# A two-layer decoder step: a 256-column matmul pair as one matmul of 512 columns

## The chip, the cores and the metric

The kernel runs on one core of one Trainium2 chip. The metric is the device time of one execution in microseconds: 1185.92 us for the kernel before (median of three runs, 1185.88 to 1188.42). All times below are from these runs and from one profiled execution.

## The reference

One inference step of a decoder with two layers: 512 prompt tokens and 8 sample tokens, 1024 channels. Layer 0 mixes tokens by attention in a window of 128, layer 1 by gated linear attention (GLA). Behind each mixer stand an output projection, a residual with layer norm, a gated feed-forward of 2816 channels with a causal convolution of width 3 on its gate half, and a second residual with layer norm. All in float32.

```python
def conv_ffn(x, buf, w_up, conv_w, conv_b, w_down):
    T = x.shape[1]
    h = x @ w_up
    a, u = h[..., :D_FF], h[..., D_FF:]
    ap = jnp.concatenate([buf.astype(a.dtype), a], axis=1)
    c = conv_b + sum(conv_w[j] * ap[:, j:j + T] for j in range(CONV_W))
    y = (jax.nn.gelu(c, approximate=False) * u) @ w_down
    return y, ap[:, T:]
...
x <- LayerNorm(ALPHA * x + mixer(x) @ w_o)
x <- LayerNorm(ALPHA * x + conv_ffn(x))
```

(The last two lines are the loop over the layers in short.) The feed-forward's weights, 1024x5632 and 2816x1024 a layer, are most of the arithmetic.

## The kernel before

Activations lie with channels on the 128 partitions and tokens along the row. The 520 tokens are two groups: a has the first 256 prompt tokens, b the other 256 and the 8 sample tokens (264). A float32 value is kept as a high and a low part in the matmul format (fp32r): xh and xl for the input of a projection, hh and hl for the hidden values or the mixer's output. Each such tile has, for each of 8 slices of 128 channels, two halves of a row of 128 (or 132) columns; `in_turn` hands the columns to the matmul one from each half in turn, and `parted` does the same split on the way in.

A weight is cut into units: 128 output channels by up to 1024 input channels. `load_unit` fetches a unit by DMA (512 KB) into raw, ACT makes its high part wh (L149), DVE its low part wl (L152). `product` (L155 to L167) is the core. For each slice k of a unit it issues three matmuls into one PSUM tile accp: wh with xh (L164), wh with xl (L165), wl with xh (L166), so a unit is 24 matmuls of 256 or 264 columns (18 in the first third of the down projection). There are four accp tiles (ACCS, L39), handed out in turn: a unit's matmuls wait until the unit four before it has been read out.

`order` (L870) sets the sequence of units: group a's and group b's units alternate, a ahead by four or five; at the start of a phase (a projection with its successors) a's first units therefore run alone. The tile framework places what each function emits on the engines in an order of its own, by a simulated timeline; on each engine that order is then fixed.

What reads the PSUM tiles:
- `out_proj` (L484) and the last third of `ffn_down` (L552) pass them to `ln_chunk` (L180): one DVE addition into the residual x (L189 or L191), a square on ACT and running sums for the layer norm. `ln_end` (L219) makes the mean and the reciprocal deviation r (L237), then for each slice u (DVE, L245), xh (ACT, L253), x (POOL, L254) and xl (DVE, L257).
- `ffn_gate` (L513): ACT copies the tile to aext (L523) and makes the first tap of the convolution from PSUM (L526); DVE adds the two other taps (L527, L528); ACT applies Gelu (L535).
- `ffn_value` (L539): DVE multiplies the gate with the PSUM tile into hprod (L543), and `split` (L169) makes hh (ACT, L170) and hl (DVE, L171).
- the other parts of `ffn_down`: one DVE addition into x (L556, L558).

The first units of a feed-forward are gate, value, gate, value and so on for group a, so the tile that the fifth unit needs is the first gate's.

Of the kernel before, what the change touches and what calls it, by code (L numbers as in the profile page):

```python
# [11 lines left out]
F32 = mybir.dt.float32  # L12
F32R = mybir.dt.float32r
I32 = mybir.dt.int32
AF = mybir.ActivationFunctionType
ALU = mybir.AluOpType
# [4 lines left out]
P = 128  # L21
D = 1024
KD = 8
# [48 lines left out]
def parted(rows):  # L72

    return rows.rearrange("p (j t) -> p t j", t=2)


def in_turn(rows):

    return rows.rearrange("p t j -> p j t")


class Group:
    def __init__(self, i):
        self.i = i
        self.n = 256 if i == 0 else 256 + NS
        self.c0 = 256 * i
        self.name = "ab"[i]


class Net:  # L90
    def __init__(self, tc, ctx, I, O):
        self.tc, self.nc, self.I, self.O = tc, tc.nc, I, O
        self.groups = [Group(0), Group(1)]
        self.stack = ctx
        pool = lambda name, bufs=1, **kw: ctx.enter_context(tc.tile_pool(name=name, bufs=bufs, **kw))
        self.const = pool("const")
        self.act = pool("act")
        self.raw = pool("raw", RAWS)
        self.wts = pool("wts", WSLOTS)
        self.ln = pool("ln")  # L100
        self.acc = pool("acc", ACCS, space=PSUM)
        self.mps = pool("mps", space=PSUM)
        self.dram = pool("dram", 2, space=DRAM)
        nc = self.nc
        c = self.const
        self.par = c.tile([P, NPAR], F32, name="par")
        self.ident = c.tile([P, P], F32, name="ident")
        self.ones_a = c.tile([P, P], F32, name="ones_a")
        nc.gpsimd.memset(self.ones_a, 1.0 / D)
        self.ones_c = c.tile([P, P], F32, name="ones_c")  # L110
        nc.gpsimd.memset(self.ones_c, 1.0 / P)
        self.eps = c.tile([P, 2], F32, name="eps")
        nc.gpsimd.memset(self.eps[:, 0:1], NORM_EPS)
        nc.gpsimd.memset(self.eps[:, 1:2], 1.0)
        for g in self.groups:
            s = [P, KD, g.n]
            g.x = self.act.tile(s, F32, name=f"x_{g.name}")

            s = [P, KD, 2, g.n // 2]
            g.xh = self.act.tile(s, F32R, name=f"xh_{g.name}")  # L120
            g.xl = self.act.tile(s, F32R, name=f"xl_{g.name}")
            g.hh = self.act.tile(s, F32R, name=f"hh_{g.name}")
            g.hl = self.act.tile(s, F32R, name=f"hl_{g.name}")
        self.units = []
        self.w = {}
# [29 lines left out]
    def product(self, g, u, rh, rl):  # L155
# [10 lines left out]
            nc.tensor.matmul(o, l[:, ks], xh, start=False, stop=k == nt - 1)  # L166
        return ps[:, :g.n]  # L167

    def split(self, hi, lo, src):  # L169
        self.nc.scalar.activation(hi, src, AF.Copy)  # L170
        self.nc.vector.tensor_tensor(lo, src, hi.bitcast(F32), op=ALU.subtract)  # L171
# [5 lines left out]
        return self.mps.tile([P, 512], F32, name=tag, bufs=2 if tag == "sc" else 1)  # L177


    def ln_chunk(self, g, m, ps, scaled):  # L180


        nc, n, x = self.nc, g.n, g.x
        t = lambda name: self.ln.tile([P, g.n], F32, name=f"{name}_{g.name}")
        c = lambda name, b=1: self.ln.tile([P, NT - 256], F32, name=name, bufs=b)[:, :n]
        if m:
            yield 0
        if scaled:
            nc.vector.tensor_tensor(x[:, m], x[:, m], ps, op=ALU.add)  # L189
        else:  # L190
            nc.vector.scalar_tensor_tensor(x[:, m], x[:, m], ALPHA, ps, op0=ALU.mult, op1=ALU.add)  # L191
        if m == 0:
            yield 1
            mp = self.mtile("sc")[:, :n]
            nc.tensor.matmul(mp, self.ones_c, x[:, 0], start=True, stop=True)
            sb = c("sb")
            nc.scalar.copy(sb, mp)
            sa = sb
            if not scaled:
                sa = c("sa")  # L200
                nc.scalar.activation(sa, mp, AF.Copy, scale=1.0 / ALPHA)
            for i in range(KD):
                eng = nc.gpsimd if i else nc.vector
                eng.tensor_tensor(x[:, i], x[:, i], sa if i else sb, op=ALU.subtract)
            g.s2 = t("s2")
            nc.scalar.activation(g.s2, x[:, 0], AF.Square)
            return
        q = c("sq", 2)
        sq = nc.scalar.activation(q, x[:, m], AF.Square)
        if m == 6 and g.i == 0:  # L210
            with self.tc.issue_after(sq.ins):
                nc.scalar.preload_act_table_set("natural_log_exp_and_others")
        if m == 1:
            g.s1 = t("s1")
        nc.vector.tensor_tensor(g.s1, x[:, 0] if m == 1 else g.s1, x[:, m], op=ALU.add)
        eng = nc.gpsimd if m < S2P else nc.vector
        eng.tensor_tensor(g.s2, g.s2, q, op=ALU.add)
# [264 lines left out]


    def out_proj(self, g, u, m, i):  # L484
        ps = self.product(g, u, g.hh, g.hl)
        yield from self.ln_chunk(g, m, ps, False)
        if m == KD - 1:
            yield from self.ln_end(g, i)

# [22 lines left out]

    def ffn_gate(self, g, u, layer, j, q):  # L513
        nc, n = self.nc, g.n
        ps = self.product(g, u, g.xh, g.xl)
        w = lambda i: self.par[:, C_CW + (layer * 3 + i) * NF + j:C_CW + (layer * 3 + i) * NF + j + 1]
        cb = self.par[:, C_CB + layer * NF + j:C_CB + layer * NF + j + 1]
        a = self.fp.tile([P, 2 + NT - 256], F32, name="aext", bufs=2)
        if g.i == 0:
            nc.gpsimd.memset(a[:, 0:2], 0.0)  # L520
        else:
            self.pcopy(a[:, 0:2], self.hist[:, j])
        nc.scalar.copy(a[:, 2:2 + n], ps)  # L523
        t = lambda name: self.fp.tile([P, NT - 256], F32, name=name, bufs=2)
        c = t("conv")
        nc.scalar.activation(c[:, :256], ps[:, :256], AF.Identity, scale=w(2), bias=cb)  # L526
        nc.vector.scalar_tensor_tensor(c[:, :256], a[:, 1:257], w(1), c[:, :256], op0=ALU.mult, op1=ALU.add)  # L527
        nc.vector.scalar_tensor_tensor(c[:, :256], a[:, 0:256], w(0), c[:, :256], op0=ALU.mult, op1=ALU.add)  # L528
        if g.i == 0:
            self.pcopy(self.hist[:, j], a[:, 256:258])  # L530
        else:
            nc.vector.scalar_tensor_tensor(c[:, 256:n], a[:, 258:2 + n], w(2), self.base[:, j], op0=ALU.mult, op1=ALU.add)
            self.pcopy(self.nconv_p[:, j], a[:, 256:258])
            self.pcopy(self.nconv_s[:, j, :, 1], a[:, 258:2 + n])
        nc.scalar.activation(c[:, :n], c[:, :n], AF.Gelu)  # L535
        g.gate = c
        yield 0

    def ffn_value(self, g, u, layer, j, q):  # L539
        nc, n = self.nc, g.n  # L540
        ps = self.product(g, u, g.xh, g.xl)
        h = self.fp.tile([P, NT - 256], F32, name="hprod", bufs=2)
        nc.vector.tensor_tensor(h[:, :n], g.gate[:, :n], ps, op=ALU.mult)  # L543
        self.split(g.hh[:, q], g.hl[:, q], parted(h[:, :n]))
        if g.i and j == NF - 1:
            nc.scalar.dma_start(out=self.O["conv_p"][layer], in_=self.nconv_p)
            nc.scalar.dma_start(out=self.O["conv_s"][layer], in_=self.nconv_s)
            self.close(self.fp_cm)
            self.fp = None
        yield 0  # L550

    def ffn_down(self, g, u, layer, part, m):  # L552
        nc = self.nc
        ps = self.product(g, u, g.hh, g.hl)
        if part == 0:
            nc.vector.scalar_tensor_tensor(g.x[:, m], g.x[:, m], ALPHA, ps, op0=ALU.mult, op1=ALU.add)  # L556
        elif part == 1:
            nc.vector.tensor_tensor(g.x[:, m], g.x[:, m], ps, op=ALU.add)  # L558
        else:
            yield from self.ln_chunk(g, m, ps, True)  # L560
            if m == KD - 1:
                yield from self.ln_end(g, 2 * layer + 1, last=layer == 1)


    def gla_open(self):
# [473 lines left out]
```

## Time and profile before

| | kernel before |
|---|---|
| runs | 1188.42, 1185.88, 1185.92 us |
| profiled execution | 1187.92 us, span 1185.1 us |
| PE busy | 1127.1 us (95%), 9598 matmuls |
| DVE busy | 777.6 us (66%) |
| ACT busy | 556.0 us (47%) |
| POOL busy | 362.0 us (31%) |
| mean granted clock of PE | 0.982 of full speed |

The span runs from the first to the last recorded instruction; the execution is longer by 2.8 us. A matmul's recorded duration overlaps the next one's, so the pace is read from start to start. PEclk is the granted clock: 1.00 is 2.4 GHz, 0.50 is 1.2 GHz. In a timeline the number in brackets is the time the engine stood idle before the instruction, and who released it.

### The profile page before, as it was taken

The numbers are of one execution on the slowest core, as the hardware profiler recorded it, in microseconds if no ns is written. First come the engines' busy times: TensorE is split into PE (matmuls) and PEld (weight loads), VectorE is DVE, ScalarE is ACT, GpSimd is POOL, SyncE is SP. The second block draws the span as 40 slices with busy tenths as digits, with TensorE's granted clock in tenths as the row PEclk, the third lists the DMA queues.
The fourth block names the chain that finished last, engine by engine and source line by source line (L and its number), as shares of the span: only waits on it lengthen the run. The fifth ranks groups of instructions, "written<-read, shape, count | busy, mean of one in ns | idle before, by whom it ended". The sixth has DMA issues, their size and how long they took to land.

```text
span 1185.1 us, 24433 instructions
## 1 busy us (share of the span) xinstructions
PE 1127.1 (95%) x9598; PEld 1088.0 (92%) x9598; DVE 777.6 (66%) x1649; ACT 556.0 (47%) x1222; POOL 362.0 (31%) x603
## 2 busy tenths in 40 slices
PE   8869989999999999999899999998999999999994
PEld 7768779899999999999799899898999999999994
DVE  7969878854555445558867678789645555355567
ACT  4447645643444234435555455456533443244433
POOL 5646676510011001147500000368210111011345
PEclk9989999999999999999899999999999999999997
DMA  7124013223323232332123553542323332323212
GB/s 224 58 82 138 2 27 123 72 81 116 108 90 108 90 107 90 107 118 95 54 72 95 160 174 121 169 127 90 94 85 119 95 107 90 107 90 107 73 61 72
DMA packets 49547, 118.57 MB, mean 100 GB/s; under 512 B 5753, under 2 KB 23321, under 8 KB 49433
## 3 DMA queue, kind: packets, MB, share of 16 engines
q1 hardware_dynamic: 47417, 115.41, 31.2%
q10 hardware_dynamic: 2016, 1.62, 0.4%
q8 instruction: 75, 1.23, 0.4%
q14 instruction: 39, 0.32, 0.1%
HBM read 108.54 MB, written 8.47 MB: 99 GB/s over the span
## 4 chain that ended last, share of the span: by engine, by line
PE 73%; DVE 12%; DMA 5%; POOL 4%; issue 3%; ACT 2%; SPq 0%; POOLq 0%; DVEq 0%; ACTq 0%
PE accp L165 22%; PE accp L164 22%; PE accp L166 22%; DMA raw<-in_w_qkv 2%; DMA vb<-dv 2%; DVE wl L152 2%; POOL x_b L254 1%; PE pv L445 1%; POOL x_a L254 1%; DVE u L245 1%; DVE qs L372 1%; DVE x_b L240 1%; DVE x_a L240 1%; PE sc L706 1%; PE pv L717 1%
## 5 line engine op out<-in xcount | busy, mean ns | idle before, releaser
L152 DVE TENSOR_TENSOR wl<-raw,wh 128x1024 fp32r<-128x1024 f32 (+2 forms) x189 | 229.1, 1213 | 142.1 <-ACT wh L149 131.6
L149 ACT ACTIVATE wh<-raw 128x1024 fp32r<-128x1024 f32 (+1 forms) x176 | 183.4, 1042 | 215.3 <-PE accp L165 191.8
L164 PE MATMUL accp<-xh_b,wh 128*128 128x264 f32 x976 | 273.5, 280 | 2.8 <-DVE hprod L543 2.8
L165 PE MATMUL accp<-xl_a,wh 128*128 128x256 f32 x976 | 271.4, 279 | 3.5 <-DVE xl_a L257 2.8
L166 PE MATMUL accp<-xh_a,wl 128*128 128x256 f32 x976 | 270.5, 278 | 3.0 <-DVE wl L152 3.0
L165 PE MATMUL accp<-xl_b,wh 128*128 128x264 f32 x976 | 272.8, 280 | 0.4 <-DVE xl_b L257 0.4
L164 PE MATMUL accp<-xh_a,wh 128*128 128x256 f32 x976 | 270.1, 279 | 3.2 <-ACT conv L526 1.4
L166 PE MATMUL accp<-xh_b,wl 128*128 128x264 f32 x976 | 272.1, 279 | 0.0
L165 PEld LDWEIGHTS accp<-xl_a,wh 128*128 128x128 f32 x976 | 187.7, 192 | 5.7 <-DVE xl_a L257 3.7
L164 PEld LDWEIGHTS accp<-xh_a,wh 128*128 128x128 f32 x976 | 187.1, 193 | 6.3 <-ACT conv L526 1.8
L166 PEld LDWEIGHTS accp<-xh_a,wl 128*128 128x128 f32 x976 | 188.1, 193 | 5.0 <-DVE wl L152 4.0
L164 PEld LDWEIGHTS accp<-xh_b,wh 128*128 128x128 f32 x976 | 186.7, 191 | 4.0 <-DVE hprod L543 3.2
L165 PEld LDWEIGHTS accp<-xl_b,wh 128*128 128x128 f32 x976 | 186.6, 191 | 1.9 <-issue 0.9
L166 PEld LDWEIGHTS accp<-xh_b,wl 128*128 128x128 f32 x976 | 186.1, 191 | 1.4 <-issue 1.3
L164 PE MATMUL accp<-hh_b,wh 128*128 128x264 f32 x480 | 133.4, 278 | 2.6 <-ACT hh_b L170 2.6
L165 PE MATMUL accp<-hl_b,wh 128*128 128x264 f32 x480 | 134.2, 280 | 0.0
L166 PE MATMUL accp<-hh_b,wl 128*128 128x264 f32 x480 | 133.3, 278 | 0.0
L165 PE MATMUL accp<-hl_a,wh 128*128 128x256 f32 x480 | 132.3, 276 | 0.3 <-DVE hl_a L171 0.3
L164 PE MATMUL accp<-hh_a,wh 128*128 128x256 f32 x480 | 132.2, 278 | 0.0
L166 PE MATMUL accp<-hh_a,wl 128*128 128x256 f32 x480 | 131.8, 275 | 0.0
L164 PEld LDWEIGHTS accp<-hh_b,wh 128*128 128x128 f32 x480 | 91.2, 190 | 3.1 <-ACT hh_b L170 2.9
L165 PEld LDWEIGHTS accp<-hl_a,wh 128*128 128x128 f32 x480 | 91.9, 192 | 1.3 <-issue 0.8
(304 smaller groups left out, 2095.6 us busy)
## 6 DMA issues: line engine op xcount, KB each, us to landing
raw<-in_w_up SPq DMA_DIRECT2D x88, 512.0 KB, 3.4
raw<-in_w_down SPq DMA_DIRECT2D x32, 512.0 KB, 3.5
raw<-in_w_gla SPq DMA_DIRECT2D x24, 512.0 KB, 3.5
raw<-in_w_mix_o SPq DMA_DIRECT2D x16, 512.0 KB, 3.9
raw<-in_w_down SPq DMA_DIRECT2D x16, 384.0 KB, 3.1
sgla<-in_state_gla SPq DMA_DIRECT2D x16, 256.0 KB, 2.8
vb<-dv SPq DMA_DIRECT2D x16, 256.0 KB, 3.9
out_gla_s<-sgla SPq DMA_DIRECT2D x16, 256.0 KB, 2.9
```

What stands on the lines that cost most here:

```text
L149: nc.scalar.activation(h[:, c], r[:, c], AF.Copy)
L152: nc.vector.tensor_tensor(l[:, c], r[:, c], h[:, c].bitcast(F32), op=ALU.subtract)
L164: nc.tensor.matmul(o, h[:, ks], xh, start=k == 0, stop=False)
L165: nc.tensor.matmul(o, h[:, ks], xl, start=False, stop=False)
L166: nc.tensor.matmul(o, l[:, ks], xh, start=False, stop=k == nt - 1)
L240: nc.vector.tensor_tensor(x[:, m], x[:, m], mu, op=ALU.subtract)
L245: nc.vector.tensor_tensor(u, x[:, m], r, op=ALU.mult)
L254: ts = nc.gpsimd.tensor_scalar(x[:, m], u, sc, bi, op0=ALU.mult, op1=ALU.add)
L372: nc.vector.tensor_tensor(qs[oth, v], r[own, :256], qs[own, v].bitcast(F32), op=ALU.subtract)
L445: nc.tensor.matmul(pv[64 * v:64 * v + 64, b * P:(b + 1) * P], self.vtok[:, kb, 64 * v:64 * v + 64], parts[v][w][:, b], start=i == 0, stop= ...
L706: nc.tensor.matmul(up, vks[b][:, 0:P], vks[b][:, P:], start=True, stop=True)
L717: nc.tensor.matmul(ob, att[:, b], vks[b][:, P:], start=first, stop=True)
```

## The change

For group a alone, in the output projections and the feed-forwards of both layers, the high and low parts lie side by side in one tile (xs_a, hs_a), and `product2` takes the place of `product`. For each slice it issues two matmuls: wh with both parts, 512 columns, into the whole PSUM tile, and wl with the high part, 256 columns, into the tile's first half. (The last slice has the two in the other order.) The second half of the tile then holds wh times the low part, and is added in a step of its own: in `ln_chunk` and `ffn_down` by another DVE addition into x; in `ffn_gate` by a DVE addition into aext, after which ACT reads aext in place of PSUM for the first tap; in `ffn_value` ACT copies it to hprod, DVE adds the other half, and the product with the gate follows. Group b, the attention's q, k and v and all GLA input projections keep `product`. The two halves that a matmul takes in turn now lie 1024 bytes apart in a row of xs_a or hs_a, where they were 512 bytes apart.

```diff
-        for g in self.groups:
+        for i, g in enumerate(self.groups):
...
+            if i == 0:
+                s = [P, KD, 2, 2, g.n // 2]
+                g.xs = self.act.tile(s, F32R, name=f"xs_{g.name}")
+                g.hs = self.act.tile(s, F32R, name=f"hs_{g.name}")
+                g.xh, g.xl = (g.xs[:, :, :, q] for q in range(2))
+                g.hh, g.hl = (g.hs[:, :, :, q] for q in range(2))
+                continue
...
+    def product2(self, g, u, rs, rh, rl):
+        if rs is None:
+            return self.product(g, u, rh, rl), None
+        nc = self.nc
+        h, l = self.w[u]
+        nt = self.units[u][1]
+        ps = self.acc.tile([P, 512], F32, name="accp")
+        o = ps.rearrange("p (j t) -> p j t", t=2)
+        for k in range(nt):
+            ks = slice(k * P, (k + 1) * P)
+            last = k == nt - 1
+            both = lambda: nc.tensor.matmul(o, h[:, ks], in_turn(rs[:, k].rearrange("p t q j -> p t (q j)")), start=k == 0, stop=last)
+            low = lambda: nc.tensor.matmul(o[:, :P], l[:, ks], in_turn(rh[:, k]), start=False, stop=False)
+            for f in (low, both) if last else (both, low):
+                f()
+        return ps[:, :256], ps[:, 256:]
...
@@ ln_chunk
+        if lo is not None:
+            nc.vector.tensor_tensor(x[:, m], x[:, m], lo, op=ALU.add)
@@ ffn_gate
-        ps = self.product(g, u, g.xh, g.xl)
+        ps, lo = self.product2(g, u, g.xs, g.xh, g.xl)
...
-        nc.scalar.activation(c[:, :256], ps[:, :256], AF.Identity, scale=w(2), bias=cb)
+        if lo is not None:
+            nc.vector.tensor_tensor(a[:, 2:2 + n], a[:, 2:2 + n], lo, op=ALU.add)
+        nc.scalar.activation(c[:, :256], ps[:, :256] if lo is None else a[:, 2:258], AF.Identity, scale=w(2), bias=cb)
@@ ffn_value
-        ps = self.product(g, u, g.xh, g.xl)
+        ps, lo = self.product2(g, u, g.xs, g.xh, g.xl)
         h = self.fp.tile([P, NT - 256], F32, name="hprod", bufs=2)
+        if lo is not None:
+            nc.scalar.copy(h[:, :n], lo)
+            nc.vector.tensor_tensor(h[:, :n], h[:, :n], ps, op=ALU.add)
+            ps = h[:, :n]
@@ ffn_down (parts 0 and 1)
+        if lo is not None:
+            nc.vector.tensor_tensor(g.x[:, m], g.x[:, m], lo, op=ALU.add)
```

In the changed kernel the lines stand lower: the addition of the gate is L557, of the value L577, the taps L559 and L560, and ln_end's r, u and xl are L267, L275 and L287.

The order on DVE at the start of layer 0's feed-forward, where group b's layer norm ends (r, u, xl_b) and the first gate (conv, aext) and value (hprod) units of group a come in; before:

```order
L237 SCALAR_TENSOR_TENSOR r<-msq,r 128x264
L245 TENSOR_TENSOR u<-x_b,r 128x264 x2
L527 SCALAR_TENSOR_TENSOR conv<-aext,par,conv 128x256 x2
L528 SCALAR_TENSOR_TENSOR conv<-aext,par,conv 128x256
L257 TENSOR_TENSOR xl_b<-x_b,xh_b 128x264
L245 TENSOR_TENSOR u<-x_b,r 128x264
```

And the same place on DVE in the changed kernel:

```order
L267 SCALAR_TENSOR_TENSOR r<-msq,r 128x264
L557 TENSOR_TENSOR aext<-aext,accp 128x256
L275 TENSOR_TENSOR u<-x_b,r 128x264 x2
L577 TENSOR_TENSOR hprod<-hprod,accp 128x256
L557 TENSOR_TENSOR aext<-aext,accp 128x256
L577 TENSOR_TENSOR hprod<-hprod,accp 128x256
L559 SCALAR_TENSOR_TENSOR conv<-aext,par,conv 128x256
```

The four additions that free PSUM tiles stand behind r now, and the taps behind them; before, DVE freed no tile here until hprod, further down, since ACT read the gates out.

The order on DVE at the start of layer 1's feed-forward, the same instructions of the same functions; before:

```order
L240 TENSOR_TENSOR x_b<-x_b,mu 128x264 x3
L235 TENSOR_TENSOR msq<-r 128x264
L236 SCALAR_TENSOR_TENSOR msq<-msq,nv 128x264
L237 SCALAR_TENSOR_TENSOR r<-msq,r 128x264
L245 TENSOR_TENSOR u<-x_b,r 128x264 x2
L527 SCALAR_TENSOR_TENSOR conv<-aext,par,conv 128x256 x2
L528 SCALAR_TENSOR_TENSOR conv<-aext,par,conv 128x256
```

And in the changed kernel:

```order
L270 TENSOR_TENSOR x_b<-x_b,mu 128x264 x3
L287 TENSOR_TENSOR xs_a<-x_a,xs_a 128x2x128 x2
L265 TENSOR_TENSOR msq<-r 128x264
L266 SCALAR_TENSOR_TENSOR msq<-msq,nv 128x264
L267 SCALAR_TENSOR_TENSOR r<-msq,r 128x264
L275 TENSOR_TENSOR u<-x_b,r 128x264 x2
L287 TENSOR_TENSOR xl_b<-x_b,xh_b 128x264
L275 TENSOR_TENSOR u<-x_b,r 128x264
L557 TENSOR_TENSOR aext<-aext,accp 128x256
```

The first gate's addition stands behind three u and an xl_b here, and the last two low parts of group a (xs_a) stand behind the x_b.

## Rows read from the trace of the kernel before

**Rows 1.** The page's table of busy time: engine, us, share, instructions.

```profile
PE 1127.1 (95%) x9598; PEld 1088.0 (92%) x9598; DVE 777.6 (66%) x1649; ACT 556.0 (47%) x1222; POOL 362.0 (31%) x603
```

**Rows 2.** The page's chain of what ended last, by engine.

```profile
PE 73%; DVE 12%; DMA 5%; POOL 4%; issue 3%; ACT 2%; SPq 0%; POOLq 0%; DVEq 0%; ACTq 0%
```

**Rows 3.** Table of stretches: us, busy time of each engine, PEclk, DMA share, GB/s.

```profile
240.00:500.00 260.00, 260.00 (x2322) 260.00 (x2322) 132.55 (x238) 106.95 (x189) 30.79 (x87) 1.00 0.32 99
```

**Rows 4.** The waits of PE: in total, times, longest, in us.

```profile
PE accp L165 <- DVE xl_a L257: 2.8, 3, 1.5
```

**Rows 5.** Timeline of PE in the dense stretch: start, duration, instruction.

```profile
236.55 0.28 PE L164 MATMUL accp<-xh_b,wh 128*128 128x264 f32 x1
...
239.25 0.27 PE L164 MATMUL accp<-xh_a,wh 128*128 128x256 f32 x1
...
241.93 0.28 PE L164 MATMUL accp<-xh_b,wh 128*128 128x264 f32 x1
```

**Rows 6.** Timeline of PE, attention of the sample columns.

```profile
160.10 0.60 PE L475 MATMUL pv<-pts,vc 128*128 128x16 f32 x4
```

**Rows 7.** Timeline of PE, f32 matmuls of the GLA layer.

```profile
597.34 0.59 PE L706 MATMUL sc<-vk 128*128 128x256 f32 x2
...
598.21 0.59 PE L717 MATMUL pv<-vk,attm 128*128 128x256 f32 x2
```

**Rows 8.** Timeline of PE, out-projection of layer 0; in brackets the idle time before.

```profile
162.82 0.45 PE L164 MATMUL accp<-hh_b,wh 128*128 128x264 f32 x1 [2.12 <-ACT hh_b L170]
```

**Rows 9.** Groups by line and form: busy us, mean ns.

```profile
L558 DVE TENSOR_TENSOR x_a<-x_a,accp 128x256 f32<-128x256 f32 x16 | 6.8, 422 | 3.3 <-PE accp L166 2.7
...
L523 ACT COPY aext<-accp 128x256 f32<-128x256 f32 x44 | 16.4, 372 | 54.1 <-PE accp L166 54.1
```

**Rows 10.** Timeline of PE, start of layer 0's feed-forward.

```profile
208.95 0.28 PE L166 MATMUL accp<-xh_a,wl 128*128 128x256 f32 x1
209.94 0.38 PE L164 MATMUL accp<-xh_a,wh 128*128 128x256 f32 x1 [0.71 <-ACT conv L526]
...
216.97 0.38 PE L164 MATMUL accp<-xh_b,wh 128*128 128x264 f32 x1 [1.40 <-DVE hprod L543]
...
223.44 0.38 PE L165 MATMUL accp<-xl_b,wh 128*128 128x264 f32 x1 [0.22 <-DVE xl_b L257]
```

**Rows 11.** Timeline of DVE, the same place.

```profile
212.00 0.43 DVE L237 SCALAR_TENSOR_TENSOR r<-msq,r 128x264 f32<-128x264 f32 x1
```

**Rows 12.** Timeline of PE, start of layer 1's feed-forward.

```profile
819.13 0.38 PE L164 MATMUL accp<-xh_a,wh 128*128 128x256 f32 x1 [0.71 <-ACT conv L526]
...
826.16 0.38 PE L164 MATMUL accp<-xh_b,wh 128*128 128x264 f32 x1 [1.41 <-DVE hprod L543]
```

**Rows 13.** Timeline of DVE, the same place.

```profile
821.71 0.78 DVE L245 TENSOR_TENSOR u<-x_b,r 128x264 f32<-128x264 f32 x2
822.40 1.03 DVE L527 SCALAR_TENSOR_TENSOR conv<-aext,par,conv 128x256 f32<-128x256 f32 x2
```

**Rows 14.** Timeline of POOL, the same place.

```profile
822.25 0.91 POOL L254 TENSOR_SCALAR x_b<-u,par 128x264 f32<-128x264 f32 x1 [1.54 <-DVE u L245]
```

**Rows 15.** Table of stretches as in rows 3, where the clock fell or stayed.

```profile
209.20:217.00 7.80, 5.68 (x50) 5.47 (x49) 7.63 (x17) 5.39 (x12) 6.27 (x11) 1.00 0.01 2
163.00:166.40 3.40, 3.40 (x23) 2.88 (x24) 1.27 (x3) 1.15 (x3) 0.83 (x3) 0.50 0.03 8
582.80:593.10 10.30, 9.76 (x35) 7.98 (x36) 5.78 (x16) 4.47 (x9) 1.05 (x2) 0.50 0.14 51
804.70:808.10 3.40, 2.85 (x13) 2.85 (x14) 3.10 (x8) 2.58 (x5) 3.40 (x3) 0.50 0.50 159
```

**Rows 16.** Table of stretches as in rows 3, the end of layer 1's out-projection.

```profile
793.00:804.00 11.00, 9.97 (x87) 9.59 (x85) 11.00 (x17) 4.88 (x9) 9.51 (x10) 1.00 0.31 108
```

**Rows 17.** Timeline of PE, attention scores of group a.

```profile
111.15 0.28 PE L396 MATMUL sc<-klo,qs 128*128 128x256 f32 x1
...
111.51 0.27 PE L164 MATMUL accp<-hh_a,wh 128*128 128x256 f32 x1
```

More of the change, by code (lines that the diff above doesn't have):

```diff
@@ L114, in __init__ @@
         nc.gpsimd.memset(self.eps[:, 1:2], 1.0)
-        for g in self.groups:
+        for i, g in enumerate(self.groups):
             s = [P, KD, g.n]
             g.x = self.act.tile(s, F32, name=f"x_{g.name}")
+            if i == 0:
[5 more added lines that the diff above has]
+                continue
             s = [P, KD, 2, g.n // 2]
+            g.xs = g.hs = None
             g.xh = self.act.tile(s, F32R, name=f"xh_{g.name}")
@@ L177, in mtile, with ln_chunk @@
         return self.mps.tile([P, 512], F32, name=tag, bufs=2 if tag == "sc" else 1)
-    def ln_chunk(self, g, m, ps, scaled):
+    def ln_chunk(self, g, m, ps, lo, scaled):
         nc, n, x = self.nc, g.n, g.x
@@ L484, in out_proj @@
     def out_proj(self, g, u, m, i):
-        ps = self.product(g, u, g.hh, g.hl)
-        yield from self.ln_chunk(g, m, ps, False)
+        ps, lo = self.product2(g, u, g.hs, g.hh, g.hl)
+        yield from self.ln_chunk(g, m, ps, lo, False)
         if m == KD - 1:
@@ L553, in ffn_down @@
         nc = self.nc
-        ps = self.product(g, u, g.hh, g.hl)
+        ps, lo = self.product2(g, u, g.hs, g.hh, g.hl)
+        if part == 2:
+            yield from self.ln_chunk(g, m, ps, lo, True)
+            if m == KD - 1:
+                yield from self.ln_end(g, 2 * layer + 1, last=layer == 1)
+            return
         if part == 0:
             nc.vector.scalar_tensor_tensor(g.x[:, m], g.x[:, m], ALPHA, ps, op0=ALU.mult, op1=ALU.add)
-        elif part == 1:
+        else:
             nc.vector.tensor_tensor(g.x[:, m], g.x[:, m], ps, op=ALU.add)
[L559 to L562, printed above, removed]
+        if lo is not None:
+            nc.vector.tensor_tensor(g.x[:, m], g.x[:, m], lo, op=ALU.add)
     def gla_open(self):
```

## The prediction

> **What bounds the kernel now.** I read the busy table of the page first: TensorE (PE) is busy 95% of the 1185.1 us span, VectorE (DVE) 66%, ScalarE (ACT) 47% [rows 1]. Then the chain of waits: 73% of it is PE, 12% DVE [rows 2]. The average hides stages, so next the table of stretches: in 240 to 500 us, inside the feed-forward of layer 0, PE is busy every one of the 260.00 us, 2322 matmuls at granted clock 1.00 (112.0 ns each), with DVE at 132.55 us (51%) and ACT at 106.95 (41%) [rows 3]. The stretch 850 to 1110 us in layer 1 reads the same. There only PE's own pace counts. Last the list of what PE waits for, and the stretches around the phase starts, where PE and DVE take turns: inside the feed-forwards those waits are few and short, the longest sort being that for xl_a [rows 4].
>
> **Part 1: the pace of the matmuls.** A unit of group a is 24 matmuls of 256 columns. It starts at 239.25 and the next starts at 241.93: 2.68 us, 111.6 ns a matmul. A unit of group b, 24 of 264 columns, takes 236.55 to 239.25: 2.70 us, 112.6 ns [rows 5]. At 2.4 GHz (clock 1.00) 264 columns are 110.0 ns, so a b matmul costs its columns plus 2.6 ns. By that, 256 columns would cost 106.7 + 2.6 = 109.3, but take 111.6. The missing 2.3 ns I read as the floor of loading a weight: the last four matmuls of 16 columns from 160.10 take 0.60 us [rows 6]; less 0.28 at most for the last one's own time (as in rows 5) that is three spacings of 107 ns or more, though 16 columns are 7 ns, so there the load sets the pace. One matmul of 512 columns is not in the trace. The nearest is an f32 matmul of 256 columns, which runs in two passes: from 597.34 to 598.21 four of them start, 0.87 us, 217.5 ns for 512 columns (to 0.01 us of the rows) [rows 7]; 512/2.4 + 2.6 is 215.9. I take 216.
>
> So a k-step (the three products of one 128-row slice of a weight) of group a takes 3 x 111.6 = 334.8 ns before. Afterwards: 216 for the 512 columns and, for the 256 columns behind it, 109.3 if the longer matmul in front lets the weight load run ahead, 111.6 if not. I take 109.3, 325.3 in all, because a load of some 110 hides easily beside 216. Saved: 9.5 ns a k-step (7.2 by the other end).
>
> The change touches (64 + 352 + 176) k-steps a layer, out, up and down projections: 1184, so 1184 matmuls go. Not all are paced by PE. The first four feed-forward units of each layer, 64 k-steps in two layers, stand in front of splits on DVE (the three waits for xl_a, 2.8 us together [rows 4]); most of the out-projection of layer 0 and some of layer 1, about 110 k-steps, end in waits for attention or GLA data, such as the 2.12 us for hh_b at 162.82 [rows 8]. About 1008 remain: 1008 x 9.5 = **-9.6 us** (-7.3 at the other end).
>
> The Trainium skill ("TensorE: Matmul & The Clock Gate", section "Back-to-back issue gap") gives N/2.4 + 2.5 ns for a warm matmul, also for 256 columns. The b rows and the f32 rows agree (112.6, 217.5); the a rows don't (111.6 against 109.2). By it the three would already cost 327.5 and only one fixed 2.5 would go, -2.5 us in place of -9.6. The measurement decides, but the same outcome stands as rival 2.
>
> **Part 2: work added beside PE.** 152 additions of 128x256 on DVE (16 + 44 + 44 + 48) at 422 ns, as the addition into x_a takes [rows 9]: 64 us of DVE. 44 copies of 372 ns on ACT [rows 9]: 16 us. In the dense stretches, which hold about four fifths of it, DVE goes from 51% to about 60%, ACT from 41% to 44%. A PSUM tile is asked for again four units later, 10.6 us, of which three units (8 us) are left after its own matmuls; an addition that waits behind one weight split and a few small operations is done in 2 to 3. I cost it at nothing there. If the cover were gone, each late tile would cost up to 0.4 us.
>
> **Part 3: the start of a feed-forward.** Here the first units of a run alone, in four PSUM tiles, while DVE is busy with group b's normalisation. Layer 0 before: the fourth unit's last matmul starts at 208.95, the fifth unit at 209.94 after a wait of 0.71 on ACT (conv, which frees the gate's tile), the first b unit at 216.97 after 1.40 on hprod [rows 10]. In the changed order the tile of the first gate is free only after the addition L557 on DVE, which stands behind r. r runs from 212.00, 0.43 us [rows 11], so L557 ends near 212.9 and the fifth unit starts at about 212.95, 3.0 us later, PE idle 3.8. The sixth follows at 215.55. The b unit then waits for its tile no longer and starts at 218.15: 1.2 us later than 216.97. Of that PE loses some in any case, since at 223.44 it waited 0.22 for the last xl_b and its first matmul then took 0.38 where 0.28 is usual [rows 10]. Net **+0.9** (0.5 to 1.2).
>
> Layer 1 before: fifth unit at 819.13, b unit at 826.16 [rows 12]. Afterwards L557 stands behind two u, an xl_b and a third u. That xl_b needs x_b from POOL, which before ran from 822.25 for 0.91, to 823.16 [rows 14]. Two u take 0.69 to the next operation at 822.40 [rows 13], a pace of 0.35; xl_b and u then end at 823.9, L557 at 824.3, the fifth unit starts at 824.4, 5.3 us late, and b at 824.4 + 2 x 2.6 = 829.6, 3.4 us late. With 0.6 back from later waits: **+2.8** (2.0 to 3.4).
>
> **Part 4: the clock.** Before, the idle 0.71 + 1.40 left the clock at 1.00 in 209 to 217 [rows 15]. After that wait of 2.12 at 162.82 [rows 8] it fell to 0.50, the 1.2 GHz level, in 163.0 to 166.4; in 582.8 to 593.1 it stayed there 10.3 us [rows 15]. An idle of 3.8 and one of 5.3 us are longer, so I expect a drop at both. In the drop at 804.7 to 808.1 PE was busy 2.85 of the 3.40 us [rows 15]; half of that is lost, 1.4. Two: **+2.8** (0 to +9.8: 9.76 busy us in the long one, 4.9 each).
>
> **Part 5: the rest.** In layer 1's out-projection DVE is full, 11.00 of 11.00 us in 793 to 804 [rows 16], and one addition stands in the chain to group a's normalisation: 0.4, with a little queueing **+0.6**; if all eight showed, at 0.34 apart, 2.7. That the scheduler places other operations of the attention and GLA ends anew I cost at nothing, within 2 us either way.
>
> **The sum** against the profiled execution, 1187.92 us (span 1185.1, 2.8 around it): -9.6 + 0.9 + 2.8 + 2.8 + 0.6 = -2.5 us. That execution is 2.0 above the median of the runs, 1185.92; from the median the forecast is **1183.4 us**. Least and most, with the bounds above except the long drops and the rivals: -9.6 + 0.5 + 2.0 + 0 + 0 - 2 = -9.1 and -7.3 + 1.2 + 3.4 + 3.4 + 2.7 + 2 = +5.4.
>
> **Rivals.**
> 1. *The starts cost little.* The clock stays up, and the later waits of the starts take in what PE lost: -9.6 + 0.5 + 2.0 + 0.6 = -6.5, 1179.4. For it: in 209 to 217 PE was busy 5.68 of 7.80 us and the clock stayed [rows 15]. Against: there the idle came in two pieces, now in one.
> 2. *Only the fixed part goes.* If the 2.3 ns belong to every 256 columns and not to the weight load, a k-step costs (2 x 111.6 - 2.6) + 111.6 = 332.2 and saves 2.6: -2.6 + 7.1 = +4.5, 1190.4. Against: the f32 passes, 217.5.
> 3. *Slower: the operand is read more slowly.* The moving columns alternate between two halves of a row; they were 512 bytes apart and become 1024. Reading has a price that depends on the order: the matmuls of L395/L396, whose 256 columns lie in one row, start 0.12 apart (111.15 to 111.51, three) [rows 17]. If 1024 bytes ran like these, a k-step would be 3 x 120 = 360, 25 ns more: 1008 x 0.025 = +25, +7 from the starts, 1218. It decides as soon as the 512-column matmul takes over 225 ns. Against: 512 (a) and 528 bytes (b) both run at one column a cycle.
> 4. *Long clock drops at both starts*, 4.9 instead of 1.4 each: +7 more, 1190.3. One long drop gives 1187.
> 5. *Much faster.* If 512 columns take no longer than 256 do in an a row, a k-step is 2 x 111.6 = 223.2 and saves 111.6: 1008 x 0.1116 = 112, and 7 from the starts, 1081. It would need two columns a cycle; the b rows, whose 8 more columns cost more, and the f32 rows speak against it [rows 5, 7]. The same page and section of the Trainium skill names about 131 ns for a sustained matmul of 512 columns; no run here shows that, and by it the time would be an estimated 1098.
>
> **How the numbers follow.** Forecast 0.50, its own range 1179.5 to 1188; rival 1 0.20; rival 2 0.08; rival 3 0.09; rival 4 0.11; rival 5 0.02. The change counts as faster below 1182.4 and as slower above 1189.5 (0.3%, 3.56 us, about what a measurement of this kernel can tell). Faster: 0.18 of the forecast, 0.18 of rival 1, 0.02: 0.38. Slower: 0.01 of the forecast, 0.05 of rival 2, 0.09 of rival 3, 0.06 of rival 4: 0.21. Same: 0.41. The range 1178 to 1191 leaves out rivals 3 and 5 and the edges of the rest.
>
> **What the changed profile would show.** Right: an a unit of 2.60 us in the dense stretch (0.216 and 0.109 in turn), PE still at 260 of 260 there; the fifth unit at the two starts 3 and 5 us late with L557 named as the releaser; a stretch at 0.50 behind each. Wrong: an a unit of 2.66 (rival 2) or 2.85 (rival 3); PE idle inside the dense stretches, waiting for L557 or L577 (part 2); no drop or a long one at the starts.

## The result, and the profile after

The changed kernel is slower: 1192.34 us against 1187.04 us for the kernel before (medians of six runs each), a ratio of 1.0049 (95% interval 1.0040 to 1.0059). The forecast was 1183.4, with 1178 to 1191. The profiled execution took 1191.58 us, its span 1189.9, 4.8 longer than the span before.

The page of the changed kernel, table of busy time and the granted clock in 40 slices:

```profile
PE 1122.1 (94%) x8414; PEld 1047.9 (88%) x8414; DVE 836.7 (70%) x1801; ACT 575.1 (48%) x1266; POOL 344.6 (29%) x603
...
PEclk9989989999999999999899999998999999999997
```

1184 matmuls are gone, 152 operations came to DVE and 44 to ACT, as worked out [rows 1]. The dense stretch, shifted by the 6 us that the kernel is late there (columns as in rows 3):

```profile
246.00:506.00 260.00, 260.00 (x1958) 249.71 (x1957) 156.84 (x294) 116.17 (x210) 23.34 (x89) 1.00 0.31 101
```

PE is still busy 260 of 260 us, DVE 60%, ACT 45%: the additions are hidden there [rows 3]. One unit of b and one of a in the timeline of PE:

```profile
247.66 0.28 PE L173 MATMUL accp<-xh_b,wh 128*128 128x264 f32 x1
...
250.35 0.38 PE L191 MATMUL accp<-xs_a,wh 128*128 128x512 f32 x1
250.57 0.27 PE L192 MATMUL accp<-xs_a,wl 128*128 128x256 f32 x1
250.68 0.38 PE L191 MATMUL accp<-xs_a,wh 128*128 128x512 f32 x1
...
252.97 0.28 PE L173 MATMUL accp<-xh_b,wh 128*128 128x264 f32 x1
```

The a unit takes 2.62 us in place of 2.68 [rows 5]: the gain is there. So the loss is elsewhere. To find it I compared the start of the same matmul (the n-th one of wl with group a's high part) in both traces; the difference is how late the changed kernel is at that point:

| point (start before, after) | late by | since the point above | forecast |
|---|---|---|---|
| first slice of layer 0's feed-forward (196.29, 199.96) | 3.7 | +3.7 | 0 |
| its eighth unit of a (228.71, 235.17) | 6.5 | +2.8 | +2.3 |
| end of its down projection (560.12, 562.48) | 2.4 | -4.1 | -4.5 |
| first slice of layer 1's output projection (748.86, 750.96) | 2.1 | -0.3 | 0 |
| first slice of layer 1's feed-forward (805.62, 813.24) | 7.6 | +5.5 | +0.6 |
| its ninth unit of a (843.28, 851.83) | 8.6 | +0.9 | +4.2 |
| end of the span (1185.1, 1189.9) | 4.8 | -3.8 | -4.5 |

Two places that the forecast held for nearly free cost 9.2 us: the end of the attention with layer 0's output projection, and the end of the GLA with layer 1's output projection and its layer norm. These are two single executions. How far one can stray shows in the four kernels named gla_out below: layer 0 issues the same operations in the same order there as before the change, and at the first slice of its feed-forward they are 0.3 us early to 1.7 late. So about half of the 3.7 may be no effect of the change; the 5.5 are beyond that. The waits of PE in the changed kernel (total, times, longest):

```profile
PE accp L191 <- DVE xs_a L287: 9.5, 4, 6.4
...
PE accp L191 <- DVE aext L557: 4.7, 2, 3.3
```

The second is the wait that the forecast expected. Of the first, 6.35 us are at the layer norm of layer 1. Timeline of PE there, in the kernel before and in the changed one:

```profile
803.25 0.49 PE L164 MATMUL accp<-xh_a,wh 128*128 128x256 f32 x2 [0.76 <-ACT xh_a L253]
805.25 0.58 PE L165 MATMUL accp<-xl_a,wh 128*128 128x256 f32 x1 [1.51 <-DVE xl_a L257]
```

```profile
806.05 0.28 PE L175 MATMUL accp<-hh_b,wl 128*128 128x264 f32 x1
812.68 0.76 PE L191 MATMUL accp<-xs_a,wh 128*128 128x512 f32 x1 [6.35 <-DVE xs_a L287]
```

ACT and DVE in the changed kernel:

```profile
799.22 0.42 ACT L263 ACTIVATE r<-nv 128x256 f32<-128x256 f32 x1
801.07 0.42 ACT L239 ACTIVATE sq<-x_b 128x264 f32<-128x264 f32 x1 [1.44 <-POOL base L539]
801.40 0.40 ACT L264 ACTIVATE r<-r 128x256 f32<-128x256 f32 x1
```

```profile
800.90 1.24 DVE L161 TENSOR_TENSOR wl<-raw,wh 128x1024 fp32r<-128x1024 f32 x1
802.07 0.97 DVE L245 TENSOR_TENSOR s_b<-s_b,x_b 128x264 f32<-128x264 f32 x1
802.96 0.72 DVE L247 TENSOR_TENSOR s_b<-s_b,sq 128x264 f32<-128x264 f32 x1
803.60 0.94 DVE L265 TENSOR_TENSOR msq<-r 128x256 f32<-128x256 f32 x1
...
807.88 0.94 DVE L267 SCALAR_TENSOR_TENSOR r<-msq,r 128x256 f32<-128x256 f32 x1
```

The same place in the kernel before, ACT and DVE:

```profile
794.46 0.42 ACT L233 ACTIVATE r<-nv 128x256 f32<-128x256 f32 x1 [1.35 <-DVE nv L232]
794.91 0.43 ACT L234 ACTIVATE r<-r 128x256 f32<-128x256 f32 x1
```

```profile
796.58 0.61 DVE L235 TENSOR_TENSOR msq<-r 128x256 f32<-128x256 f32 x1
...
801.41 0.41 DVE L237 SCALAR_TENSOR_TENSOR r<-msq,r 128x256 f32<-128x256 f32 x1
```

From the first r on ACT to r on DVE it is 7.0 us before and 8.7 after, and it starts 4.8 us later. Between the two r on ACT now stands a square of group b, and the second r waits behind it until 801.40. DVE has the same kind of move: a weight split and two sums of group b stand ahead of the first msq. This second move is the one that counts most: r is done on ACT at 801.80, and DVE comes to msq only at 803.60. So msq starts 4.4 us after the first r, where it was 2.1. No added operation is in that stretch; the scheduler has placed the old ones otherwise. In the clock's stretches (columns as in rows 15) the drop in layer 0's output projection and that before layer 1's feed-forward are twice as long as before, and one has come at 217.8 (the one in the GLA is shorter, 586.4 to 593.2 for 582.8 to 593.1 [rows 15]). The length of the first one is not the change's doing alone: in gla_out_6_moved, whose layer 0 is as before, it is 6.8 us too (162.7 to 169.6).

```profile
159.80:166.60 6.80, 6.80 (x26) 6.08 (x26) 5.01 (x15) 2.18 (x8) 5.56 (x11) 0.50 0.00 0
217.80:221.20 3.40, 3.40 (x13) 2.95 (x12) 3.40 (x10) 2.78 (x6) 2.26 (x4) 0.50 0.00 0
811.70:818.50 6.80, 5.82 (x18) 5.02 (x19) 6.50 (x14) 4.02 (x7) 6.80 (x6) 0.50 0.49 158
```

### The profile page after: what moved, and what is told of

Its sections match the earlier page's. It is cut to its first block, busy times and chain, and to the rows that moved or that the text cites. A ratio compares the mean times of both kernels' runs of the same rounds, so it can differ in the third digit from the quotient of the medians.

```text
span 1189.9 us, 22246 instructions
## 1 busy us (share of the span) xinstructions
PE 1122.1 (94%) x8414; PEld 1047.9 (88%) x8414; DVE 836.7 (70%) x1801; ACT 575.1 (48%) x1266; POOL 344.6 (29%) x603
## 4 chain that ended last, share of the span: by engine, by line
PE 74%; DVE 12%; DMA 6%; issue 3%; POOL 2%; ACT 2%; SPq 0%; ACTq 0%; POOLq 0%; DVEq 0%
PE accp L191 19%; PE accp L174 13%; PE accp L173 13%; PE accp L175 13%; PE accp L192 10%; DMA raw<-in_w_qkv 3%; DMA vb<-dv 2%; DVE wl L161 2%; POOL x_a L284 1%; DVE qs L402 1%; ACT pr L448 1%; DVE x_b L270 1%; DVE u L275 1%; DVE sgla L823 1%; DVE x_a L270 1%
## 5 line engine op out<-in xcount | busy, mean ns | idle before, releaser
L191 PE MATMUL accp<-xs_a,wh 128*128 128x512 f32 x704 | 245.3, 389 | 14.5 <-DVE xs_a L287 9.5
L192 PE MATMUL accp<-xs_a,wl 128*128 128x256 f32 x704 | 179.8, 276 | 0.0
L191 PE MATMUL accp<-hs_a,wh 128*128 128x512 f32 x480 | 167.4, 389 | 0.7 <-DVE sg L840 0.7
L191 PEld LDWEIGHTS accp<-xs_a,wh 128*128 128x128 f32 x704 | 135.0, 192 | 31.9 <-issue 7.9
L192 PEld LDWEIGHTS accp<-xs_a,wl 128*128 128x128 f32 x704 | 136.7, 194 | 2.6
L192 PE MATMUL accp<-hs_a,wl 128*128 128x256 f32 x480 | 123.7, 278 | 0.1
L191 PEld LDWEIGHTS accp<-hs_a,wh 128*128 128x128 f32 x480 | 91.6, 192 | 11.6 <-DVE sg L840 1.0
L192 PEld LDWEIGHTS accp<-hs_a,wl 128*128 128x128 f32 x480 | 92.7, 194 | 3.1 <-issue 0.9
L174 PEld LDWEIGHTS accp<-hl_b,wh 128*128 128x128 f32 x480 | 90.7, 189 | 2.3 <-DVE hl_b L199 0.6
L202 POOL COPY hist<-aext 128x2 f32<-128x2 f32 x44 | 9.0, 205 | 286.3 <-DVE aext L557 286.3
```

What stands on the lines that cost most here:

```text
L174: nc.tensor.matmul(o, h[:, ks], xl, start=False, stop=False)
L191: both = lambda: nc.tensor.matmul(o, h[:, ks], in_turn(rs[:, k].rearrange("p t q j -> p t (q j)")), start=k == 0, stop=last)
L192: low = lambda: nc.tensor.matmul(o[:, :P], l[:, ks], in_turn(rh[:, k]), start=False, stop=False)
```

## The experiments

Ratios are to the kernel before, run beside each, with 95% intervals. Theory A: the output projections cost, through the order. Theory B: the starts of the feed-forwards.

**out_single.** `out_proj` passes None in place of g.hs, and so uses three matmuls.

```diff
-        ps, lo = self.product2(g, u, g.hs, g.hh, g.hl)
+        ps, lo = self.product2(g, u, None, g.hh, g.hl)
```

> Group a's output projections of both layers go back to the three-matmul product; the feed-forwards keep the 512-column matmuls. Theory A (the loss comes from the output projections: their extra additions make the scheduler place the attention's and GLA's end and the layer norm of group a in another order): the 3.6 us lost by the end of layer 0's output projection and most of the 5.5 us lost before layer 1's feed-forward go, 0.5 of matmul pace with them: about 1184.5 us against 1187.0 before, i.e. 0.2% faster than before. Theory B (the loss is made at the starts of the feed-forwards, where the first 512-column matmul needs both parts and the tiles are freed late by the addition on DVE): hardly changed, 1190 to 1192.

Measured 1185.82 us, 0.9983 (0.9972 to 0.9994): A. Without the output projections' part the change is a small gain.

**out_double_only.** The same edit in ffn_gate, ffn_value and ffn_down instead.

> The reverse: only group a's output projections use the 512-column matmuls, the feed-forwards keep three. Theory A: the loss of some 8 us stands without the feed-forward's gain of 7 to 8: about 1194 us. Theory B: the output projections are harmless, 1187 us (within 1).

Measured 1196.13 us, 1.0071 (1.0056 to 1.0085): the output projections alone, 64 slices a layer, cost 8 us. A, as expected.

**start_single** and **out_start_single.** The first six units of each feed-forward use three matmuls, by this edit in ffn_gate and ffn_value; in the second kernel the output projections do too:

```diff
-        ps, lo = self.product2(g, u, g.xs, g.xh, g.xl)
+        ps, lo = self.product2(g, u, g.xs if j >= 3 else None, g.xh, g.xl)
```

> As the changed kernel, but the first six units of group a in each feed-forward (j below 3) use three matmuls and give their tiles free as before. Theory A: only the starts' own cost goes, 2.8 in layer 0 and 1 in layer 1: about 1188.5 us. Theory B: all of the loss at the starts and behind the layer norms goes: about 1183 us. In both, no wait for L557 at the starts and no clock drop at 218 us.

> Both together: output projections and the first six units of each feed-forward with three matmuls. Theory A: 1187.0 less about 900 slices times 7.5 ns (6.8): 1180 to 1181 us, 0.5% faster than before. Theory B gives the same as with the first six units alone, about 1183.

Measured 1187.67 us, 1.0002 (0.9992 to 1.0011), and 1180.67 us, 0.9946 (0.9934 to 0.9958). Both are on A's side: the starts cost some 5 us, more than the 3.8 that A gave them, the output projections 7 to 8, and without both the gain of the dense stretches, 0.54%, is left.

**gate_start_single.** What of a start costs? Output projections single, and the edit above in ffn_gate alone.

> Single output projections; in the feed-forwards only the first three gate units of group a (j below 3) use three matmuls, the value units all use the 512-column form. So the first gates' PSUM tiles are read out by ACT alone, as before, while three of the first six units still need both parts at their start. If the late release of the gates' tiles by L557 on DVE makes the cost of the starts (5.1 us between out_single and out_start_single), the time is that of out_start_single within 1.5 us: 0.994 to 0.996. If the need for both parts at once makes it, about half of the 5.1 us stays: 0.997.

Measured 1180.67 us, 0.9941 (0.9929 to 0.9954): all of the starts' cost goes, though the value units still need both parts. It is the tile that L557 frees late. PE at the fifth unit of both layers, first in out_single, then in gate_start_single:

```profile
214.02 0.79 PE L191 MATMUL accp<-xs_a,wh 128*128 128x512 f32 x1 [3.82 <-DVE aext L557]
...
822.35 0.48 PE L191 MATMUL accp<-xs_a,wh 128*128 128x512 f32 x1 [3.66 <-DVE aext L557]
```

```profile
209.74 0.38 PE L173 MATMUL accp<-xs_a,wh 128*128 128x256 f32 x1 [0.60 <-ACT conv L558]
...
815.49 0.38 PE L173 MATMUL accp<-xs_a,wh 128*128 128x256 f32 x1 [0.60 <-ACT conv L558]
```

And the clock behind it, out_single and gate_start_single:

```profile
212.30:219.10 6.80, 5.08 (x16) 4.44 (x17) 6.66 (x18) 4.74 (x8) 4.20 (x8) 0.50 0.00 0
```

```profile
209.00:217.00 8.00, 7.23 (x50) 6.30 (x50) 7.83 (x18) 6.02 (x13) 5.42 (x9) 1.00 0.01 3
```

**adds_only.** Are the additions to blame without any 512-column matmul? The kernel before with 16 operations more, which take the larger of x and itself and so leave it as it is; in ln_chunk:

```diff
             nc.vector.scalar_tensor_tensor(x[:, m], x[:, m], ALPHA, ps, op0=ALU.mult, op1=ALU.add)
+            if g.i == 0:
+                nc.vector.tensor_tensor(x[:, m], x[:, m], x[:, m], op=ALU.max)
```

> The kernel before, with 16 further DVE operations of 128x256 (x_a is replaced by the larger of itself and itself, which leaves it as it is) behind group a's additions in both output projections; all matmuls stay as before. The scheduler moves layer 1's layer norm as in the changed kernel. Theories A1 and A2: 4 to 8 us slower than before, without any 512-column matmul. If instead the 512-column matmul itself is to blame (it needs both parts at its start), the same time as before, within 1 us.

Measured 1194.75 us, 1.0057 (1.0041 to 1.0074): the additions suffice. In its trace 2.6 us are lost by the first slice of layer 0's feed-forward and 5.1 between the last slices of layer 1's output projection and its feed-forward, but only 1.3 at the GLA's end (772.63 to 780.84 of the kernel before), where out_double_only lost over 5. The 2.6 are not far beyond what single executions stray by there. In the layer norm, ACT and then DVE:

```profile
801.07 0.42 ACT L235 ACTIVATE r<-nv 128x256 f32<-128x256 f32 x1 [0.25 <-DVE nv L234]
801.52 0.42 ACT L236 ACTIVATE r<-r 128x256 f32<-128x256 f32 x1
803.71 0.42 ACT L211 ACTIVATE sq<-x_b 128x264 f32<-128x264 f32 x1 [1.78 <-DVE x_b L191]
```

```profile
803.60 1.41 DVE L152 TENSOR_TENSOR wl<-raw,wh 128x1024 fp32r<-128x1024 f32 x1
...
805.82 0.95 DVE L237 TENSOR_TENSOR msq<-r 128x256 f32<-128x256 f32 x1
```

Here the two r on ACT stand together, and the loss is made all the same: msq waits behind the weight split on DVE. Group b's square on ACT is not needed for it.

**gla_out_7_kept** and **gla_out_7_moved.** Work or order? Only layer 1's output projection has the 512-column matmuls, in seven units of eight; the feed-forwards use three. The moved kernel has `m != 3` in place of `m != 6`:

```diff
-        ps, lo = self.product2(g, u, g.hs, g.hh, g.hl)
+        ps, lo = self.product2(g, u, g.hs if i == 2 and m != 6 else None, g.hh, g.hl)
```

> Only layer 1's output projection of group a uses the 512-column matmuls, and only seven of its eight units (all but m = 6). With this choice the scheduler keeps the order of the kernel before in group a's layer norm behind it: nv, the x_a subtractions, one x_b addition, msq, s_b, msq, one weight split, s_b, r on DVE, and the two r operations back to back on ACT. Theory A1 (the order is what costs): within 1 us of the kernel before, though seven additions are made. Theory A2 (the additions' own time on the busy DVE costs): seven eighths of the 5.6 us lost there, 4.9 us slower than before.

> The same with seven of eight units, but m = 3 left out in place of m = 6. The work on every engine is the same as with m = 6 left out; but here the scheduler puts a square of group b between the two r operations on ACT, and a weight split and two s_b additions ahead of the first msq on DVE. Theory A1: 4.5 to 5.6 us slower than before. Theory A2: 4.9 us slower, and the same as with m = 6 left out.

Measured 1.0029 (1.0019 to 1.0038) and 1.0054 (1.0040 to 1.0068). The pair does equal work and differs by 3 us, so order counts. But A1 alone expected the first within 1 us of before: 3.3 us remained. ACT in the kept and in the moved one:

```profile
797.83 0.42 ACT L263 ACTIVATE r<-nv 128x256 f32<-128x256 f32 x1 [0.91 <-DVE nv L262]
798.28 0.42 ACT L264 ACTIVATE r<-r 128x256 f32<-128x256 f32 x1
```

```profile
800.99 0.40 ACT L263 ACTIVATE r<-nv 128x256 f32<-128x256 f32 x1
802.58 0.43 ACT L239 ACTIVATE sq<-x_b 128x264 f32<-128x264 f32 x1 [1.20 <-DVE x_b L219]
802.91 0.40 ACT L264 ACTIVATE r<-r 128x256 f32<-128x256 f32 x1
```

The kept one is 1.4 us early at slice 773.97 of the kernel before and 4.8 late at 780.84: it loses at the GLA's end, and next to nothing behind it. There both have the PE order of the changed kernel, but the moved one loses more, with a drop of 6.8 us at 780.8 for one of 3.4 at 780.5. Other DVE operations have changed places there too. So the 3 us between the two are not the layer norm's order alone. For that order the stretch from the first r on ACT to r on DVE tells more. In all fifteen traces it is 6.4 to 7.3 us where no weight split stands ahead of msq (nine of them) and 8.1 to 8.9 where one does (six).

**gla_out_6_kept** and **gla_out_6_moved.** For that place: six units, `i == 2 and m >= 2` and `i == 2 and m < 6`. Both keep the layer norm's order.

> Only layer 1's output projection of group a uses the 512-column matmuls, six of its eight units (m = 2 to 7). The layer norm's order is that of the kernel before, and PE has done 246, 252 and 267 of group a's slices ahead of the GLA's last matmuls (before: 246, 252, 264). If PE's order is what costs at the GLA's end: 0 to 1.5 us slower than before (0.9995 to 1.0013). If the additions' own time costs: 6/8 of what all eight units cost in layer 1 (5.6), 4.2 us slower.

> The same with six units, but m = 0 to 5: the layer norm's order again as before, the work on each engine the same as with m = 2 to 7, but PE has done 250, 258 and 274 slices ahead of the GLA's last matmuls, as in the changed kernel. If PE's order costs: 3 to 4 us slower than before (1.0025 to 1.0034), with PE idle some 2 us for hh_b behind 776 us. If the additions' own time costs: the same as with m = 2 to 7, or less, since no addition stands in the chain to the layer norm here.

Measured 1187.83 us, 1.0001 (0.9992 to 1.0010), and 1191.37 us, 1.0028 (1.0017 to 1.0040), against 1187.67 before: equal work, some 3 us apart, as PE's order expects. PE in the kept one: the GLA's last product of keys and values (sc<-vk), then the stretch of the output projection (columns as in rows 3).

```profile
755.94 0.70 PE L745 MATMUL sc<-vk 128*128 128x256 f32 x2
```

```profile
776.00:784.00 8.00, 7.97 (x62) 7.50 (x62) 6.84 (x16) 4.88 (x11) 1.90 (x2) 1.00 0.53 115
```

The same in the moved one:

```profile
758.64 0.70 PE L745 MATMUL sc<-vk 128*128 128x256 f32 x2
...
780.38 0.69 PE L173 MATMUL accp<-hh_b,wh 128*128 128x264 f32 x2 [1.94 <-ACT hh_b L198]
```

```profile
780.50:783.90 3.40, 3.32 (x11) 2.54 (x12) 2.73 (x6) 2.66 (x5) 0.00 (x0) 0.50 0.69 132
```

More of group a's slices stand ahead of that product, which comes 2.7 us later; then group a's work is used up, PE waits 1.94 us for hh_b, and the clock falls. DVE's order differs between the two in the same stretch, so PE's is the likely cause and not the only one left.

**out_11_kept** and **out_11_start_single.** Both layers with `m >= (3 if i == 0 else 2)`, 11 of 16 units; the second with the dense feed-forward and single starts.

> Only output projections use the 512-column matmuls, 11 of the 16 units of group a: m = 3 to 7 in layer 0, m = 2 to 7 in layer 1. With this choice the scheduler keeps three places as in the kernel before: the attention's last softmaxes and hl_b on DVE, the number of group a's slices that PE does ahead of the GLA's last matmuls (246, 252 and 264; the changed kernel has 250, 258 and 274), and group a's layer norm in layer 1. Theory A1 (order): within 1 us of the kernel before, i.e. a ratio of 0.999 to 1.001. Theory A2 (the additions' own time): 11/16 of the 8.1 us that all 16 units cost, 5.6 us slower.

> The feed-forwards with 512-column matmuls from the seventh unit on, and the same 11 units of the output projections. Theory A1: the 88 slices of the output projections add at most 88 x 7.5 ns = 0.7 us of gain to the 6.4 us of the kernel with single output projections and starts: 0.994, the same as that kernel within 1 us. Theory A2: about 5 us slower than that kernel, 0.998 to 0.999.

Measured 1.0014 (1.0005 to 1.0023) and 0.9943 (0.9931 to 0.9956). Against 5.6 us by A2, 1.7 us are left; A1's bound is missed by a little. The second is the same as out_start_single.

**split_512.** The changed kernel with each 512-column matmul as two of 256 columns:

```diff
-            both = lambda: nc.tensor.matmul(o, h[:, ks], in_turn(rs[:, k].rearrange("p t q j -> p t (q j)")), start=k == 0, stop=last)
+            def both():
+                nc.tensor.matmul(o[:, :P], h[:, ks], in_turn(rh[:, k]), start=k == 0, stop=False)
+                nc.tensor.matmul(o[:, P:], h[:, ks], in_turn(rl[:, k]), start=False, stop=last)
```

> The changed kernel with each 512-column matmul issued as two of 256 columns into the two halves of the same PSUM tile: the layout, the additions and copies stay, only the saving on PE goes. If the pace of PE gains 7.5 ns a slice in the dense stretches, as the two traces show, 1192.3 + 1008 x 0.0075 = about 1200 us (1198 to 1202), an a unit of 2.68 us. If reading halves 1024 bytes apart were slower than 512, an a unit above 2.72 us and over 1204 us.

Measured 1197.01 us, 1.0072 (1.0052 to 1.0091), below the 1198 to 1202 expected. Its dense stretch:

```profile
246.00:506.00 260.00, 260.00 (x2322) 260.00 (x2321) 154.00 (x291) 113.86 (x206) 23.06 (x88) 1.00 0.32 99
```

2322 matmuls as before [rows 3], so halves 1024 bytes apart are read at the old pace, and none of the 7 us is gained. Its PE order at the GLA's end is that of the kernel before, and it loses 1.5 us there (772.63 to 780.84) instead of 4.4: a miss of mine, since I kept the changed kernel's order in the sum.

## Why the prediction was wrong

**Part 1 (pace)** was right in its mechanism and a little too high. An a unit takes 2.62, not 2.60 us: 0.218 + 0.109 a slice. The 512 columns take 218 ns, where I took 216 from 512/2.4 + 2.6. The 217.5 of the f32 rows was only as sharp as rows of 0.01 us: to the nanosecond those four starts are 216 apart, and they are two f32 matmuls of the program with two records each, not four. Gained in the stretches of the table, from the eighth and ninth unit on: 4.1 + 3.8 = 7.9 us, against 9.0 forecast for them. By the Trainium skill ("TensorE: Matmul & The Clock Gate", section "Back-to-back issue gap") 512 columns would take 215.8 ns by its formula; the trace is 2 ns above that, and far from the 131 ns that it gives for a sustained stream. Rivals 2, 3 and 5 fell with the a unit of 2.62 us, rival 1 with the cost of the starts; rival 4's drops of 10 us did not come there.

**Part 2 (cover)** was right: no wait inside the dense stretch.

**Parts 3 and 4 (starts, clock)** were right in mechanism: PE waits for L557 in both layers, 3.29 us at 216.66 and 1.45 at 830.23, with a drop of 3.4 us behind the first. 6.5 us were forecast; 3.7 were lost in the changed kernel, where in layer 1 the delay in front had probably taken the place of part of the wait. In out_single, without that delay, the fifth units wait 3.82 and 3.66 us, where an idle of 3.8 and 5.3 was forecast. The clock falls there at both starts, for 6.8 and 3.4 us, and the loss is about 5.

**Part 5 is the step that failed.** "That the scheduler places other operations of the attention and GLA ends anew I cost at nothing, within 2 us either way", and +0.6 for the additions on a full DVE: measured 3.7 + 5.5 in the traces, and 7 to 8 by the runs with and without the output projections' part. I had read the changed order at the starts of the feed-forwards only. The orders at the two mixers' ends and at layer 1's norm were as readable. In layer 1 they have three moves: group b's square between the two r on ACT; a weight split and two sums ahead of msq on DVE; and on PE more of group a's slices of hh ahead of the GLA's last matmuls, 250, 258 and 274 for 246, 252 and 264 (240 of them belong to layer 0). The split on DVE goes with a norm's stretch that is 1 to 2 us longer (8.1 to 8.9 for 6.4 to 7.3). The square adds little: the stretch is 8.1 us in the two traces that have the split without it (adds_only, split_512) and 8.6 to 8.9 in the four with both. PE's order goes with 3 us in the six-unit pair. What the additions cost by their own time is under 2 us where the order stays (1.0001 with 6 units, 1.0014 with 11).

Open: layer 0's part. The traces give 3.7 us to its attention end and output projection in the changed kernel, 2.2 in out_double_only and 2.6 in adds_only. Kernels whose layer 0 is as before come up to 1.7 late at the same slice, with a drop as long as here. By the runs, both layers' output projections cost 1.0071 and layer 1's alone, with seven units, 1.0054; the 2 us between them are not clear of the noise, since the two intervals overlap. What is left for layer 0 was not separated into the additions' own time and order.

## What to carry to other kernels

With a scheduler that orders by a simulated timeline, a few operations on a busy engine can cost more by what they move than by what they take: compare the order of every engine at each phase end, not only where the edit stands. Where parts of a change can be left out one by one, pick those that leave the order as it was; gate_start_single, with the feed-forwards' gain alone, runs in 0.9941 of the time before. And ask of a PSUM tile which engine frees it last, and what that engine has queued in front.

## What had not been expected of the hardware

The length of the last wait did not decide on the clock. It fell to 0.50 behind a single wait of 1.94 us (780.38 in gla_out_6_moved), and in adds_only at 565.0 behind three, of which the longest was 0.85. It stayed at 1.00 behind one of 1.71 us at 780.95 in the changed kernel, and behind two of 0.71 and 1.40 us [rows 10, 15]. A 256-column matmul behind one of 512 columns starts the next after 109 ns, where it is 111.6 in a row of its kind; of the two 256-column matmuls at the end of an a unit, both take 109.
